# Partition sums of the modulation partials on TensorE, GpSimd's additions on VectorE, and a fourth raw weight buffer

## The chip, the core and the metric

The kernel runs on one core of a Trainium2 chip. The metric is the device time of one execution in microseconds (us). The engines are TensorE (PE, its weight loads PEld), VectorE (DVE), ScalarE (ACT), GpSimd (POOL) and SyncE (SP), which here only issues DMAs.

## The reference

One layer of a diffusion backbone in float32 over 128 context tokens and 256 latent tokens (384 columns together), width 2048:

```
mod = silu(c) @ w_ada + b_ada           # six parts of 2048: sh1, sc1, gt1, sh2, sc2, gt2; two vectors c (context, latent)
h   = RMSNorm(x) * (1 + sc1) + sh1
proj = h @ w_in                         # q, k, v, f, u, vg, three gates
merged = sum_i sigmoid(gate_i) * (branch_i @ w_br_i)     # attention, Fourier, spatial gating
x  += gt1 * RMSNorm(merged @ w_out)
h   = RMSNorm(x) * (1 + sc2) + sh2
x  += gt2 * RMSNorm(relu(h @ w1)^2 @ w2)
```

Weights lie in HBM in float32. `mod` is a product of two vectors with a matrix of 2048 x 12288.

## The kernel before

Weights come through one stream. `stream` is a list of entries of 512 KB: ("W", ...) entries are split into a high part (fp32r) and the low part that is left, ("D", ...) entries are handed to a function. `emit_dma` issues the entry's load on SP's queue into one of `R_BUFS` = 3 tiles `raw`; a tile comes free when the last instruction that reads it is done. `advance` takes the next entry. For a "W" entry it makes two half-tiles, each with a `whi` (ScalarE's cast, L71) and a `wlo` (VectorE's subtraction, L72, recorded under the helper's line L65); there are `H_BUFS` = 4 of each. `next_half` gives TensorE one half-tile, and looks ahead until two more are made. Each product is three matmuls (`mm3`, L575 to L577, or `mmB1`, L598 to L600), so a half-tile is 12 matmuls of 384 columns.

A "D" entry of `ada_dve` is worked on VectorE: for both vectors v it multiplies 128x512 weights by a column of `silT` (per-partition scalar) and adds to an accumulator (L271, L274), four instructions for an entry. After eight entries (2048 rows) the accumulator holds 128 partial sums of each column, one in each partition, which have still to be added over the partitions. These entries are mixed into the stream: sixteen of `CORR` ("v0" and "f": the shift's share of two projections) with the first main entries, twelve blocks `ADA(m, j)` of m = 2, 4, 3 with the gates and the output projection, four of m = 5 (gt2) with the first part of the MLP.

The sum over the partitions is GpSimd's `partition_all_reduce` (`all_sum`), which leaves it in all partitions. For m = 2, 3, 4 the result is wanted as a column (`modT`, features in partitions): a mask keeps the diagonal (`affine_select`) and `fin` reduces it on VectorE (L304). GpSimd also adds the gated branches (`br_evac`, L1059) and the squares of x before the MLP (`x2_d`, L1194).

The order on every engine is that of the program. After each half-tile `slot()` runs a task or two of the lists `late` (evacuations), `urgent` and `side`; `delayed` holds tasks that become urgent some slots later (`RED_AFTER`, `ADD_AFTER`).

Of the kernel before, what the change touches and what calls it, by code (L numbers as in the profile page):

```python
# [13 lines left out]
F32 = mybir.dt.float32  # L14
F32R = mybir.dt.float32r
# [20 lines left out]
def hybrid_layer_kernel(ctx: ExitStack, tc: tile.TileContext, I: dict, O: dict):  # L36
# [250 lines left out]
    def mod_done(m, j):  # L287
        s = slice(4 * j, 4 * j + 4)

        def one(v):  # L290
            def run():
                t = adr["t"][:, 1, j % 2, v, :]
                all_sum(t, accs[m, j][v])
                t3 = t.rearrange("p (n k) -> p n k", n=4)
                nc.gpsimd.affine_select(out=t3, in_=t3, pattern=[[0, 4], [1, P]], base=0, channel_multiplier=-1,
                                        compare_op=ALU.is_equal, fill=0.0)
                if v == 1:
                    accs.pop((m, j))
                    nc.gpsimd.load_library(library_config.standard)
            return run  # L300
# [11 lines left out]
        def tasks():  # L312
            delayed.append([RED_AFTER, [fin]])
            return [one(0), one(1)]
        return tasks
# [3 lines left out]
    def gt2_done(j):  # L319
        c = slice(512 * j, 512 * (j + 1))  # L320

        def one(v):
            def run():
                acc = accs[5, j][v]
                if "t" not in a2bc:
                    a2bc["t"] = area.tile([P, 2, D], F32, tag="a2", name="a2")
                a2 = a2bc["t"]
                if v == 0:
                    for q, src in enumerate((I["b_ada"][0:1, 5 * D + 512 * j:5 * D + 512 * (j + 1)],
                                             I["g_post_mlp"][0:1, c])):  # L330
                        a2bc[j, q] = tp.tile([P, 512], F32, tag="sq", name=f"bg{j}{q}")
                        nc.gpsimd.dma_start(out=a2bc[j, q], in_=src.to_broadcast([P, 512]))
                all_sum(a2[:, v, c], acc)
                if v == 1:
                    accs.pop((5, j))
                    if j == 3:
                        nc.gpsimd.load_library(library_config.standard)
# [12 lines left out]
    def corr_done(name):  # L350
        def one(v):
# [1010 lines left out]
```

## Time and profile before

| | us |
|---|---|
| median of 3 runs | 2242.39 (2242.16 to 2245.22) |
| profiled execution, first to last instruction | 2241.9 |
| TensorE busy | 2168.3 (97%) |
| VectorE busy | 1458.1 (65%) |
| ScalarE busy | 814.8 (36%) |
| GpSimd busy | 252.6 (11%) |

The profiled execution is 0.5 us shorter than the median, so its parts can be read as parts of the run's time. Its stretches are: to about 180 the first entries, to 420 the rest of q, k, v and the spatial gating, to about 1000 gates and branches (`g`, `b`), to 1148 the output projection (`y`), to 1211 the first blocks of the MLP while its input is made, then the MLP. Busy time of TensorE is modelled and matmuls overlap, so what its idle time and the granted clock tell is read by stretch. The clock column is the mean share of full speed that was granted: 1.00 is the 2.4 GHz level, 0.50 the 1.2 GHz one.

### The profile page before, as it was taken

To read this page: it belongs to the slowest core of one execution; us is meant where nothing else is said; L and a number is where in the kernel's file an instruction comes from. 1 tells how busy PE (TensorE), PEld (TensorE's weight loads), DVE (VectorE), ACT (ScalarE), POOL (GpSimd) and SP (SyncE) were. 2 spreads that over 40 slices of the span, in tenths; PEclk is the share of its full clock that TensorE was granted. 3 is DMA by queue.
4 is the path that set the end of the run, shared out by engine and by line. 5 is a ranking of instruction groups with operands and counts; after the bars stand their busy time and mean duration, and the time that the engine had idled before them with its cause. 6 is when DMAs were issued, how large, how long until landed. Compare 5 with 4: busy or idle time off the path is not lost.

```text
span 2241.9 us, 30677 instructions
## 1 busy us (share of the span) xinstructions
PE 2168.3 (97%) x11479; PEld 1988.6 (89%) x11479; DVE 1458.1 (65%) x2331; ACT 814.8 (36%) x1602; POOL 252.6 (11%) x167
## 2 busy tenths in 40 slices
PE   7999899999999998999999999999999999999998
PEld 3679888999899998998989988899889998899986
DVE  4445675558998898989977577787444444345454
ACT  3332334533223232323245443344333443334441
POOL 0000221011222122212212001111000000000000
PEclk9999999999999999999999999999999999999999
DMA  8897753336666765666634466665444444444452
GB/s 309 288 314 232 198 161 123 103 116 196 201 195 194 212 207 168 201 203 224 218 102 134 126 191 200 205 188 174 127 132 124 128 125 129 126 130 123 123 175 88
DMA packets 284405, 387.29 MB, mean 173 GB/s; under 512 B 16156, under 2 KB 184304, under 8 KB 283872
## 3 DMA queue, kind: packets, MB, share of 16 engines
q1 hardware_dynamic: 275952, 372.82, 53.6%
q10 hardware_dynamic: 6192, 6.77, 1.0%
q0 software_dynamic: 2112, 5.74, 0.9%
q8 instruction: 90, 1.47, 0.3%
q14 instruction: 59, 0.48, 0.1%
HBM read 377.94 MB, written 8.26 MB: 172 GB/s over the span
## 4 chain that ended last, share of the span: by engine, by line
PE 75%; DVE 9%; DMA 8%; issue 5%; ACT 1%; POOL 1%; DVEq 0%; ACTq 0%; POOLq 0%; SPq 0%
PE m L576 7%; PE m L577 7%; PE m L575 7%; PE z L599 7%; PE z L600 7%; PE z L598 7%; DMA raw<-in_w_in_dram 4%; DVE wlo L65 4%; PE g L577 3%; PE g L575 3%; PE g L576 3%; DVE adr L274 3%; DMA raw<-in_w_ada_dram 2%; PE sc L248 2%; PE ew L598 1%
## 5 line engine op out<-in xcount | busy, mean ns | idle before, releaser
L65 DVE TENSOR_TENSOR wlo<-raw,whi 128x512 fp32r<-128x512 f32 x908 | 649.7, 734 | 573.5 <-ACT whi L71 566.2
L71 ACT CAST whi<-raw 128x512 fp32r<-128x512 f32 x908 | 547.8, 620 | 1102.8 <-PE z L600 262.0
L598 PE MATMUL z<-whi,ff 128*128 128x512 f32 x720 | 280.1, 389 | 0.0
L599 PE MATMUL z<-wlo,ff 128*128 128x512 f32 x720 | 280.1, 389 | 0.0
L600 PE MATMUL z<-whi,ff 128*128 128x512 f32 x720 | 280.1, 389 | 0.0
L274 DVE SCALAR_TENSOR_TENSOR adr<-raw,silT,adr 128x512 f32<-128x512 f32 x360 | 266.8, 801 | 15.5 <-DMA raw<-in_w_ada_dram 15.4
L577 PE MATMUL g<-hA,wlo 128*128 128x384 f32 x768 | 261.5, 341 | 15.6 <-DVE wlo L65 15.3
L575 PE MATMUL g<-hA,whi 128*128 128x384 f32 x768 | 260.9, 340 | 10.5 <-ACT whi L71 10.5
L576 PE MATMUL g<-hA,whi 128*128 128x384 f32 x768 | 259.4, 338 | 0.0
L575 PE MATMUL m<-h2a,whi 128*128 128x386 f32 x512 | 175.1, 342 | 2.1 <-ACT h2a L1181 2.1
L576 PE MATMUL m<-h2a,whi 128*128 128x386 f32 x512 | 174.3, 340 | 1.1 <-DVE h2a L1185 1.0
L577 PE MATMUL m<-h2a,wlo 128*128 128x386 f32 x512 | 173.8, 339 | 0.0
L577 PEld LDWEIGHTS g<-hA,wlo 128*128 128x128 f32 x768 | 146.2, 190 | 22.1 <-DVE wlo L65 22.1
L600 PEld LDWEIGHTS z<-whi,ff 128*128 128x128 f32 x720 | 135.1, 188 | 28.0
L598 PEld LDWEIGHTS z<-whi,ff 128*128 128x128 f32 x720 | 135.1, 188 | 27.9
L599 PEld LDWEIGHTS z<-wlo,ff 128*128 128x128 f32 x720 | 135.1, 188 | 27.9
L575 PEld LDWEIGHTS g<-hA,whi 128*128 128x128 f32 x768 | 146.1, 190 | 11.5 <-ACT whi L71 11.4
L576 PEld LDWEIGHTS g<-hA,whi 128*128 128x128 f32 x768 | 146.2, 190 | 0.0
L281 POOL PARTITION_ALL_REDUCE adr<-adr x24 | 87.4, 3640 | 302.8 <-DVE adr L274 235.1
L576 PEld LDWEIGHTS m<-h2a,whi 128*128 128x128 f32 x512 | 97.3, 190 | 2.3 <-DVE h2a L1185 2.1
L575 PEld LDWEIGHTS m<-h2a,whi 128*128 128x128 f32 x512 | 97.1, 190 | 2.4 <-ACT h2a L1181 2.3
L577 PEld LDWEIGHTS m<-h2a,wlo 128*128 128x128 f32 x512 | 96.9, 189 | 0.0
(343 smaller groups left out, 3824.6 us busy)
## 6 DMA issues: line engine op xcount, KB each, us to landing
raw<-in_w_mlp_dram SPq DMA_DIRECT2D x244, 512.0 KB, 3.7
raw<-in_w_in_dram SPq DMA_DIRECT2D x156, 512.0 KB, 3.8
raw<-in_w_ada_dram SPq DMA_DIRECT2D x128, 512.0 KB, 4.5
erb<-in_w_ada_dram SPq DMA_DIRECT2D x37, 512.0 KB, 5.5
raw<-in_w_out_dram SPq DMA_DIRECT2D x32, 512.0 KB, 4.2
era<-in_w_ada_dram SPq DMA_DIRECT2D x27, 512.0 KB, 5.1
era<-in_w_in_dram SPq DMA_DIRECT2D x20, 512.0 KB, 5.4
raw<-in_w_br_a_dram SPq DMA_DIRECT2D x16, 512.0 KB, 3.6
```

The costliest lines, as they stand in the source:

```text
L65: eng.tensor_tensor(out=out, in0=a, in1=b, op=op)
L71: nc.scalar.copy(out=hi, in_=full)
L248: nc.tensor.matmul(ps[g:g + 2, :wd], silT[:, :, k], r, start=k < 4, stop=k >= KT - 4)
L274: nc.vector.scalar_tensor_tensor(out=acc[v], in0=r, scalar=vec[:, v, k:k + 1], in1=acc[v], op0=ALU.mult, op1=ALU.add)
L281: nc.gpsimd.partition_all_reduce(out, acc, P, bass_isa.ReduceOp.add)
L575: nc.tensor.matmul(out, wh, xh, start=start, stop=False)
L576: nc.tensor.matmul(out, wh, xl, start=False, stop=False)
L577: nc.tensor.matmul(out, wl, xh, start=False, stop=stop)
L598: nc.tensor.matmul(ps[t], xh, hi, start=first, stop=False)
L599: nc.tensor.matmul(ps[t], xh, lo, start=False, stop=False)
L600: nc.tensor.matmul(ps[t], xl, hi, start=False, stop=last_)
```

## The change

The sums over the partitions become matmuls with ones. For m = 2, 3, 4, `red` multiplies each 128x128 piece of an accumulator (as weights) by one column of ones: eight matmuls of one column leave the sums in a PSUM tile in the layout of `modT`, and `fin` adds the bias from there. For m = 5 and `CORR`, `sum_bc` multiplies a 128x128 of ones by the accumulator, 512 columns, and leaves the sum in all partitions; the following addition on VectorE reads it from PSUM. `red` becomes urgent four slots after the last accumulation. The additions of `br_evac` and `x2_d` go to VectorE. `R_BUFS` is 4. The accumulators of `CORR` and of m = 5 lie in other tiles, and no GpSimd library is loaded.

```
-    R_BUFS = 3
+    R_BUFS = 4
     H_BUFS = 4
-    RED_AFTER = 14
-    ADD_AFTER = 7
+    RED_AFTER = 4
...
-                delayed.append([1, on_done()])
+                delayed.append([RED_AFTER, on_done()])
...
-    def all_sum(out, acc):
-        nc.gpsimd.partition_all_reduce(out, acc, P, bass_isa.ReduceOp.add)
+    def sum_bc(acc):
+        pb = mis_tile("sum")
+        nc.tensor.matmul(pb, ones, acc, start=True, stop=True)
+        return pb
...
-        def one(v):
-            def run():
-                t = adr["t"][:, 1, j % 2, v, :]
-                all_sum(t, accs[m, j][v])
-                t3 = t.rearrange("p (n k) -> p n k", n=4)
-                nc.gpsimd.affine_select(out=t3, in_=t3, pattern=[[0, 4], [1, P]], base=0, channel_multiplier=-1,
-                                        compare_op=ALU.is_equal, fill=0.0)
...
+        def red():
+            pr = mis_tile(f"red{m}{j}")
+            for v, acc in enumerate(accs.pop((m, j))):
+                for n in range(4):
+                    nc.tensor.matmul(pr[:, 4 * v + n:4 * v + n + 1], acc[:, n * P:(n + 1) * P], ones[:, 0:1],
+                                     start=True, stop=True)
+            last["red"] = pr
 
         def fin():
             dst = modT[:, m, :, s]
-            nc.vector.tensor_reduce(out=dst, in_=adr["t"][:, 1, j % 2].rearrange("p v (n k) -> p v n k", n=4),
-                                    axis=AX.X, op=ALU.add)
-            tt(nc.vector, dst, dst, bc2(bT[:, m, s]), ALU.add)
+            tt(nc.vector, dst, last.pop("red")[:, 0:8].rearrange("p (v n) -> p v n", v=2), bc2(bT[:, m, s]), ALU.add)
...
-        return lambda: [one(0), one(1), nop, nop, nop, fin]
+        return lambda: [load, nop, nop, red(0), add(0), red(1), add(1), fin]
...
+        def red():
+            pc.extend(sum_bc(acc) for acc in accs.pop((name, 0)))
 
         def add():
             dst, after = evacuated[name]
             for t in range(NT):
-                tt(nc.vector, dst[:, t, :], dst[:, t, :], evacuated["t"][min(t, 1)], ALU.add)
+                tt(nc.vector, dst[:, t, :], pc[min(t, 1)], dst[:, t, :], ALU.add)
...
                 if gi:
-                    tt(nc.gpsimd, sigs[0, n], sigs[0, n], s, ALU.add)
+                    tt(nc.vector, sigs[0, n], sigs[0, n], s, ALU.add)
...
-            tt(nc.gpsimd, sq2, sq2, sq, ALU.add)
+            tt(nc.vector, sq2, sq2, sq, ALU.add)
```

GpSimd before, at the second pair of column blocks: the four additions of gated branches of this pair (`sig`; numbers are buffers), then the library's load and the first partition sum of the next block.

```order
L65 TENSOR_TENSOR sig_4382<-sig_4382,sig_4542 128x384
L65 TENSOR_TENSOR sig_4396<-sig_4396,sig_4556 128x384
L65 TENSOR_TENSOR sig_4382<-sig_4382,sig_4696 128x384
L65 TENSOR_TENSOR sig_4396<-sig_4396,sig_4710 128x384
L281 ISA
L281 ISA adr<-adr 128x512
```

None of these rows is left on GpSimd: the additions stand on VectorE, the sums on TensorE, and the mask and the library loads (the bare `ISA` rows) are gone.

VectorE before, at the same pair, from the half-tile behind the Fourier branch (`b_..4757` and `4758` are its two products):

```order
L65 TENSOR_TENSOR sig_4542<-b_1_0_4757,sig_4542 128x384
L65 TENSOR_TENSOR sig_4556<-b_1_1_4758,sig_4556 128x384
L65 TENSOR_TENSOR wlo_0_4852<-raw_4803,whi_0_4851 128x512
L65 TENSOR_TENSOR wlo_1_4856<-raw_4803,whi_1_4855 128x512
L65 TENSOR_TENSOR sig_4696<-b_1_0_4801,sig_4696 128x384
L65 TENSOR_TENSOR sig_4710<-b_1_1_4802,sig_4710 128x384
```

VectorE now, at the same place (`4755` and `4756` are those products):

```order
L64 TENSOR_TENSOR sig_4545<-b_1_0_4755,sig_4545 128x384
L64 TENSOR_TENSOR sig_4385<-sig_4385,sig_4545 128x384
L64 TENSOR_TENSOR modT<-red_4799,bT 128x2x4
L64 TENSOR_TENSOR a_93<-modT,vT 128x2x4
L64 TENSOR_TENSOR sig_4559<-b_1_1_4756,sig_4559 128x384
L64 TENSOR_TENSOR sig_4399<-sig_4399,sig_4559 128x384
L64 TENSOR_TENSOR wlo_0_4861<-raw_4763,whi_0_4860 128x512
L64 TENSOR_TENSOR wlo_1_4865<-raw_4763,whi_1_4864 128x512
L64 TENSOR_TENSOR sig_4699<-b_1_0_4808,sig_4699 128x384
L64 TENSOR_TENSOR sig_4385<-sig_4385,sig_4699 128x384
L64 TENSOR_TENSOR sig_4713<-b_1_1_4809,sig_4713 128x384
L64 TENSOR_TENSOR sig_4399<-sig_4399,sig_4713 128x384
```

Each product is now followed by an addition, and `fin` of the block m = 2, j = 0 (the rows that write `modT` and `a_93`) stands between them, where a reduce of 128x1024 stood some rows later.

TensorE at the same place, before: the last matmuls of the Fourier branch and the first of the next.

```order
L576 MATMUL b_1_1_4758<-oF,whi_1_4724 128x384
L577 MATMUL b_1_1_4758<-oF,wlo_1_4725 128x384
L575 MATMUL b_1_0_4801<-oC,whi_0_4767 128x384
L576 MATMUL b_1_0_4801<-oC,whi_0_4767 128x384
```

TensorE now:

```order
L568 MATMUL b_1_1_4756<-oF,whi_1_4727 128x384
L569 MATMUL b_1_1_4756<-oF,wlo_1_4728 128x384
L300 MATMUL red_4799<-ones,adr 128x1 x8
L567 MATMUL b_1_0_4808<-oC,whi_0_4765 128x384
L568 MATMUL b_1_0_4808<-oC,whi_0_4765 128x384
```

Eight one-column matmuls stand between two half-tiles, behind the half `wlo_1_4728`. VectorE makes that half behind the last accumulation of the block, as its rows now show:

```order
L278 SCALAR_TENSOR_TENSOR adr<-raw_4635,silT,adr 128x512 x4
L64 TENSOR_TENSOR wlo_0_4724<-raw_4641,whi_0_4723 128x512
L64 TENSOR_TENSOR wlo_1_4728<-raw_4641,whi_1_4727 128x512
L275 TENSOR_SCALAR adr<-raw_4677,silT 128x512 x2
```

The last row begins the next block, in the other pair of accumulators.

SP's queue before, at the first loads of the main stream (each row with the semaphores that it waits for: a DMA's, or VectorE's when a buffer has to come free):

```order
L97 DMA raw_1315<-in_w_in_dram 128x4x256
L97 DMA raw_1321<-in_w_in_dram 128x2x512
L97 DMA raw_1363<-in_w_in_dram 128x4x256 [waits DMAHW0_49]
L97 DMA raw_1522<-in_w_in_dram 128x4x256 [waits DMAHW6_49,DMAHW3_49,DVE_49]
L97 DMA raw_1530<-in_w_in_dram 128x2x512 [waits DMAHW7_49,DMAHW4_49,DVE_49]
L97 DMA raw_1566<-in_w_in_dram 128x4x256 [waits DMAHW5_49,DMAHW0_49,DVE_49]
```

SP's queue now:

```order
L95 DMA raw_1315<-in_w_in_dram 128x4x256
L95 DMA raw_1321<-in_w_in_dram 128x2x512
L95 DMA raw_1363<-in_w_in_dram 128x4x256 [waits DMAHW0_49]
L95 DMA raw_1417<-in_w_in_dram 128x4x256 [waits DMAHW1_49]
L95 DMA raw_1524<-in_w_in_dram 128x2x512 [waits DMAHW6_49,DMAHW4_49,DVE_49]
L95 DMA raw_1531<-in_w_in_dram 128x4x256 [waits DMAHW7_49,DMAHW5_49,DVE_49]
```

The fourth load no longer waits for VectorE, and each later one waits for the buffer that is released one load earlier than before.

## Rows read from the trace of the kernel before

**Rows 1.** Stretches (us): busy time and (count) of each engine, granted clock, DMA share, GB/s.
```profile
0.00:180.00 180.00, 165.13 (x878) 111.12 (x879) 83.56 (x204) 67.42 (x120) 3.99 (x13) 1.00 0.87 296
180.00:300.00 120.00, 109.94 (x600) 104.20 (x599) 80.69 (x133) 34.71 (x70) 20.41 (x19) 0.97 0.71 210
300.00:540.00 240.00, 239.57 (x1345) 226.59 (x1344) 143.51 (x258) 100.93 (x211) 27.95 (x23) 1.00 0.44 134
540.00:1150.00 610.00, 576.66 (x3221) 563.45 (x3219) 531.73 (x757) 181.31 (x337) 141.50 (x76) 0.98 0.65 198
1150.00:1215.00 65.00, 58.56 (x316) 55.91 (x316) 53.91 (x102) 34.06 (x78) 20.50 (x19) 0.95 0.39 116
1215.00:2241.90 1026.90, 1018.40 (x5130) 927.29 (x5128) 564.67 (x880) 396.35 (x790) 38.24 (x17) 1.00 0.47 144
```

**Rows 2.** What TensorE waited for: total us, times, longest; 540 to 1150, then 180 to 300.
```profile
PE g L577 <- DVE wlo L65: 15.3, 15, 3.7
PE g L575 <- ACT whi L71: 10.5, 2, 8.6
...
PE q L575 <- ACT whi L71: 5.9, 3, 3.7
```

**Rows 3.** ScalarE's waits in 540 to 1150, the one on GpSimd.
```profile
ACT mH L1063 <- POOL sig L65: 25.4, 6, 12.5
```

**Rows 4.** GpSimd's groups in 540 to 1150: busy us, mean ns | idle before.
```profile
L281 POOL PARTITION_ALL_REDUCE adr<-adr x24 | 87.4, 3640 | 302.8 <-DVE adr L274 235.1 <-ACT whi L71 49.2 <-issue 12.6
L65 POOL TENSOR_TENSOR sig<-sig,sig 128x384 f32<-128x384 f32 x28 | 34.5, 1254 | 173.3 <-DVE sig L65 158.7 <-issue 7.5 <-DVE wlo L65 7.1
```

**Rows 5.** VectorE's groups in 540 to 1150, same columns.
```profile
L274 DVE SCALAR_TENSOR_TENSOR adr<-raw,silT,adr 128x512 f32<-128x512 f32 x338 | 251.7, 804 | 15.0 <-DMA raw<-in_w_ada_dram 14.8
L65 DVE TENSOR_TENSOR wlo<-raw,whi 128x512 fp32r<-128x512 f32 x266 | 200.4, 791 | 48.2 <-ACT whi L71 46.0 <-PE g L577 1.3
L271 DVE TENSOR_SCALAR adr<-raw,silT 128x512 f32<-128x512 f32 x22 | 30.3, 1419 | 0.4 <-DMA raw<-in_w_ada_dram 0.4
L65 DVE TENSOR_TENSOR sig<-b,sig 128x384 f32<-128x384 f32 x42 | 21.3, 547 | 0.0
L304 DVE TENSOR_REDUCE modT<-adr 128x8 f32<-128x1024 f32 x12 | 14.5, 1210 | 0.0
```

**Rows 6.** Same tiles, whole span: duration ns min/median/max, first and last start us.
```profile
L274 DVE SCALAR_TENSOR_TENSOR adr<-raw,silT,adr x360: 733/744/2728, 508.3 to 1111.8; 128x512 f32<-128x512 f32 x180
L271 DVE TENSOR_SCALAR adr<-raw,silT x24: 473/1062/2468, 507.5 to 1071.7; 128x512 f32<-128x512 f32 x24
...
L65 DVE TENSOR_TENSOR wlo<-raw,whi x908: 674/691/2733, 187.5 to 2201.1; 128x512 fp32r<-128x512 f32 x182
```

**Rows 7.** Seven stretches without GpSimd work: the last one, and their sum.
```profile
1080.00:1110.00 30.00, 29.29 (x166) 28.26 (x166) 28.08 (x49) 9.46 (x18) 0.00 (x0) 1.00 0.74 230
...
sum 180.00, PE 178.91 PEld 176.96 DVE 157.45 ACT 57.10 POOL 0.24; mean PE 25.56 PEld 25.28 DVE 22.49 ACT 8.16 POOL 0.03
```

**Rows 8.** Three pieces at the lower clock: the first and the last.
```profile
659.00:668.00 9.00, 5.27 (x17) 5.28 (x18) 7.95 (x10) 1.46 (x3) 4.69 (x2) 0.62 0.51 164
...
968.00:975.00 7.00, 5.23 (x21) 4.91 (x20) 6.13 (x10) 1.91 (x4) 1.54 (x2) 0.76 0.59 179
```

**Rows 9.** TensorE in time around `colsum`: start us, us, what.
```profile
1207.89 0.34 PE L577 MATMUL m<-h2c,wlo 128*128 128x386 f32 x1
1208.07 0.72 PE L1126 MATMUL r<-ones,sq 128*128 128x1 f32 x6
...
1208.92 0.33 PE L576 MATMUL m<-h2c,whi 128*128 128x386 f32 x1
```

**Rows 10.** TensorE in time around L491, same columns.
```profile
24.57 0.81 PE L491 MATMUL pr<-dg,ones 128*128 128x384 f32 x2
25.31 0.60 PE L248 MATMUL sc<-erb,silT 128*2 128x512 f32 x2
```

**Rows 11.** DMA before the main stream, columns as in group 1.
```profile
173.00:186.00 13.00, 13.00 (x76) 13.00 (x76) 5.76 (x13) 7.32 (x15) 1.54 (x3) 1.00 0.11 34
```

More of the change, by code (lines that the diff above doesn't have):

```diff
@@ L8 @@
 import concourse.tile as tile
-from concourse import bass_isa, library_config
 from concourse import mybir
@@ L260, in run @@
                     if "t" not in adr:
-                        adr["t"] = area.tile([P, 2, 2, 2, 512], F32, tag="a2", name="adr")
-                    accs[m, j] = [adr["t"][:, 0, j % 2, v, :] for v in range(2)]
-                else:
-                    accs[m, j] = [tp.tile([P, 512], F32, tag="ada", name=f"ada{m}_{j}_{v}", bufs=3) for v in range(2)]
+                        adr["t"] = area.tile([P, 2, 2, 512], F32, tag="a2", name="adr")
+                    accs[m, j] = [adr["t"][:, j % 2, v, :] for v in range(2)]
+                elif m == 5:
+                    if "t" not in a2bc:
+                        a2bc["t"] = area.tile([P, 2, D], F32, tag="a2", name="a2")
+                    accs[m, j] = [a2bc["t"][:, v, 512 * j:512 * (j + 1)] for v in range(2)]
+                else:
+                    if "t" not in evacuated:
+                        evacuated["t"] = area.tile([P, 2, 2, 512], F32, tag="B2a", name="corr")
+                    accs[m, j] = [evacuated["t"][:, int(m == "f"), v, :] for v in range(2)]
             acc = accs[m, j]
@@ L310, in fin @@
                 plus1_times(A2, 4, g_pre_mlp, s)
[L312 to L315, printed above, removed]
+        return lambda: [red, fin]
     a2bc = {}
@@ L320, in gt2_done, with load, red, add @@
         c = slice(512 * j, 512 * (j + 1))
-        def one(v):
-            def run():
[L324 to L337, printed above, removed]
+        def load():
+            for q, src in enumerate((I["b_ada"][0:1, 5 * D + 512 * j:5 * D + 512 * (j + 1)],
+                                     I["g_post_mlp"][0:1, c])):
+                a2bc[j, q] = tp.tile([P, 512], F32, tag="sq", name=f"bg{j}{q}")
+                nc.gpsimd.dma_start(out=a2bc[j, q], in_=src.to_broadcast([P, 512]))
+        def red(v):
+            def run():
+                a2bc["ps"] = sum_bc(accs[5, j][v])
+            return run
+        def add(v):
+            def run():
+                tt(nc.vector, a2bc["t"][:, v, c], a2bc.pop("ps"), a2bc[j, 0], ALU.add)
             return run
         def fin():
-            for q, op in enumerate((ALU.add, ALU.mult)):
-                tt(nc.vector, a2bc["t"][:, :, c], a2bc["t"][:, :, c],
-                   a2bc[j, q].unsqueeze(1).to_broadcast([P, 2, 512]), op)
-        return lambda: [one(0), one(1), nop, nop, nop, fin]
+            accs.pop((5, j))
+            tt(nc.vector, a2bc["t"][:, :, c], a2bc["t"][:, :, c],
+               a2bc[j, 1].unsqueeze(1).to_broadcast([P, 2, 512]), ALU.mult)
+        return lambda: [load, nop, nop, red(0), add(0), red(1), add(1), fin]
     def ADA(m, j):
@@ L350, in corr_done @@
     def corr_done(name):
-        def one(v):
-            return lambda: all_sum(evacuated["t"][v], accs[name, 0][v])
+        pc = []
+        def red():
+            pc.extend(sum_bc(acc) for acc in accs.pop((name, 0)))
         def add():
@@ L356, in add @@
             for t in range(NT):
-                tt(nc.vector, dst[:, t, :], dst[:, t, :], evacuated["t"][min(t, 1)], ALU.add)
-            accs.pop((name, 0))
+                tt(nc.vector, dst[:, t, :], pc[min(t, 1)], dst[:, t, :], ALU.add)
             after()
-        def tasks():
-            delayed.append([ADD_AFTER, [add]])
-            return [one(0), one(1)]
-        return tasks
+        return lambda: [red, nop, add]
     evacuated = {}
@@ L704, in hybrid_layer_kernel @@
     oA = area.tile([P, 2, 8, 386], F32R, tag="B1", name="oA")
-    oF = area.tile([P, 2, 4, 386], F32R, tag="B2a", name="oF")
+    oF = {}
     at2 = area.tile([P, 8 * 386], F32, tag="B2b", name="att2")
@@ L793, in run @@
             assert f_ready
+            if not oF:
+                oF["t"] = area.tile([P, 2, 4, 386], F32R, tag="B2a", name="oF")
             c = slice(g * P, (g + 1) * P)
@@ L826, in run @@
                 tt(nc.vector, fo[:, t0 + n - 1:t0 + h:-1], cc, ss, ALU.subtract)
-            put_o(fo, oF, g)
+            put_o(fo, oF["t"], g)
         return run
@@ L1038, in hybrid_layer_kernel @@
     src_m = lambda p, k: mt[p][:, k, :]
[L1039 removed]
+    src_o = lambda p, k: oA[:, p, k, :] if k < 8 else oF["t"][:, p, k - 8, :] if k < 12 else gt["o"][:, p, k - 12, :]
     sigs = {}
```

6 lines of the change are left out of this document (removed).

## The prediction

> **What bounds the kernel now.** I read the stretches first, to see who is full where [rows 1]. TensorE (PE) is full in two of them: 239.6 of 240 us busy from 300 to 540, and all but 8.5 of 1026.9 us from 1215 on. It waits in three: the start (14.9 us, which no edit touches), 180 to 300 (10.1 us), and 540 to 1150, the gates, branches and output projection (33.3 us idle). Only that third stretch also has VectorE (DVE) nearly full, 531.7 of 610 us, beside 141.5 us of GpSimd (POOL). So the next view is what ended TensorE's waits [rows 2]: in 540 to 1150 it is the low weight halves that VectorE makes (`wlo`, L65, 15 waits of gate matmuls, 15.3 us) and the high halves of ScalarE (`whi`, L71, 10.5 us in two waits, one of 8.6). The 8.6 has GpSimd behind it: ScalarE itself waited 25.4 us in this stretch for sums of gated branches from GpSimd, 12.5 us once [rows 3], and every later `whi` stands behind that instruction.
>
> Then GpSimd's and VectorE's groups in the same stretch [rows 4, 5]. The three costliest VectorE groups are slower here than the same forms elsewhere [rows 6]: 338 accumulations at a mean of 804 ns against a median of 744, 266 `wlo` at 791 against 691, 22 first products at 1419 against a minimum of 473. That is 338 x 0.060 + 266 x 0.100 + 22 x 0.946 = 20.3 + 26.6 + 20.8 = 67.7 us of VectorE time, lost beside 141.5 us of GpSimd, 0.48 us for each us. Where GpSimd is quiet, TensorE hardly waits: in seven stretches of 180 us with 0.24 us of GpSimd it is idle 1.1 us [rows 7].
>
> One more loss: after a wait the granted clock falls to the lower level, and TensorE is busy but at half pace. At full pace a matmul of this stage takes 29.29 / 166 = 0.176 us [rows 7]. Three pieces of the stretch have a mean granted clock of 0.62 to 0.76; in the first, 17 matmuls took 5.27 us, 2.3 us too long, in the last, 21 took 5.23, 1.5 too long [rows 8]. About 6 us in the three. So 33.3 + 6 = 39 us is all that 540 to 1150 can give.
>
> **The change, part by part.**
> *What leaves GpSimd in 540 to 1150.* All 24 all-reduces, their masks and 28 of the 32 branch sums [rows 4]. VectorE loses 67.7 us of slowdown and twelve reduces (14.5 us [rows 5]), and gains 28 adds of 128x384. The same form costs it 547 ns [rows 5], so 15.3 us. It comes to 531.7 - 67.7 - 14.5 + 15.3 = 465 us of some 600: no longer late on the mean. ScalarE's wait for GpSimd goes too, since the add now stands ahead of `hi` on VectorE, one 0.55 us instruction. I expect TensorE to wait as it does beside a quiet GpSimd: 1.1 / 180 of some 570 us, 3.5 us. The worst of those stretches has 0.71 us in 30 [rows 7], which would be 13.5. So 39.2 - 3.5 = 35.7 us come back; the bounds are 25.7 and 39.2.
>
> *What is added on TensorE.* Twelve `red` of eight one-column f32 matmuls each. The nearest rows are the three of `colsum` [rows 9], same shape and type: from the ordinary matmul before them (1207.89) to the second one after them (1208.92) is 1.03 us, two ordinary steps of which are 0.35, so 0.68 us for three, 0.226 each, and 96 cost 21.7 us. They lie wholly in 540 to 1150. Twelve `sum` matmuls of 128x512 f32 with ones: the nearest is the 128x384 one of L491, which runs as two records and holds TensorE from 24.57 to 25.31, 0.74 us [rows 10]; by columns 0.99 for 512, so 11.8 us. Unscaled it would be 8.9; at two whole records of 0.60, as the next row's 512-column ones have, 14.4. I take 11.8, the same kind of operand. Four lie before 540 and eight behind 1215, where TensorE has no idle time to hide them. Together 33.5 us.
>
> *The waits that these make.* `red` waits for VectorE's last accumulation, and all of TensorE is behind it. It is issued four half-tiles after that accumulation, and the low halves that TensorE used in between stand behind the accumulation in VectorE's order, so it is done: 0. `fin` on VectorE waits for `red`, with the next `wlo` behind it; TensorE then has two half-tiles in stock, 24 matmuls or 4.2 us, against `fin` and two `wlo` of 0.69: 0 as well, while VectorE has spare time. If that cover is gone, each `red` shows as a wait of TensorE for `wlo`.
>
> *The fourth raw buffer.* Around 180 the DMA engines are idle: 0.11 busy from 173 to 186 [rows 11], since the three raws allowed behind the early entries have been asked for. A fourth now lands there. Sixteen `CORR` entries stand among the first 26 main ones, so 1.6 raws go with the 24 matmuls (4.2 us) of one, and one raw more is a lead of 2.6 us, against three waits of 5.9 us in `q`, the longest 3.7 [rows 2]. The stretch has 10.1 us idle and a granted clock of 0.97 [rows 1], two half-pace pieces that I put at 3 us. At most 13 us, at least nothing, since the DMA engines are 0.71 busy there and some transfers would only queue. I take 6. In 540 to 1150 its help is in the 35.7.
>
> *The additions behind 1150.* Fifteen adds of 128x384 move to VectorE, 15 x 0.547 = 8.2 us, into 65 us of which it works 53.9 [rows 1]. On GpSimd they were 15 x 1.25 us [rows 4], 19 of its 20.5 us there, and by the rate above these cost VectorE 0.48 x 19 = 9. Zero, within 3 either way. (The `bg` rows of m = 5 stay on GpSimd's queue, issued four slots ahead of the addition that reads them, in a stage where VectorE works 564.7 of 1026.9 us: 0.)
>
> *Sum.* 2241.9 - 35.7 - 6 + 33.5 + 0 = 2233.7 us of the profiled execution; the runs' median lies 0.5 above its span, so **2234 us**. With every bound at its good end 2241.9 - 39.2 - 13 + 30.6 - 3 = 2217, at its bad end 2241.9 - 25.7 + 36.1 + 3 = 2255. The change swaps some 42 us of waiting for some 33 us of matmuls.
>
> **The rivals.**
> *TensorE pays and is not paid back: slower.* The 33.5 us are certain; the return is not. If VectorE stays late, because the adds fall on the very slots at the branch blocks' ends where it has most to do (two products, two adds and two low halves in three half-tiles), half of the 39.2 us comes back: 2241.9 - 19.6 - 0 + 33.5 = 2256, or 2250 with the buffer's 6. It decides at a return of 33.5 us over both stretches. For it: VectorE is the last releaser in most waits [rows 2]. Against: 465 of 600 us, and the quiet stretches, where VectorE is as busy. The Trainium skill has a rule on this side (GPSIMD Engine Reference, Engine selection): a reduction along the partitions is given to GpSimd. By it the sums stay where TensorE pays nothing; this case's row has 3.64 us for one 128x512 all-reduce against 1.8 us for two accumulators' `red`, so the trace has the cheaper sum on TensorE, though on the engine that is full.
> *The buffer gives nothing: no change.* The DMA engines are the limit from 188 to 270, and the rest goes as forecast: 2241.9 - 35.7 + 33.5 = 2239.7, 2240 in the runs.
> *Everything comes back.* 39 and 13 us, 2241.9 - 52.2 + 33.5 = 2223.
> *`red` waits for VectorE.* If the four half-tiles are too few, twelve waits as long as the longest for `wlo` now, 3.7 us [rows 2], 44 us: over 2270. The order of the instructions speaks against it.
>
> **How the numbers follow.** The forecast has 0.50, everything back 0.10, the buffer without effect 0.23, slower 0.17 (0.03 of it the wait of `red`). Differences under 0.2% (4.5 us) can hardly be told from none here. Faster (under 2238) is the forecast and the good case, 0.60; the same is the third, 0.23; slower 0.17. The likeliest case's own range is 2226 to 2238. A range from 2222 to 2250 leaves out the far end of the slower case and a little below.
>
> **What would show it.** In the profile after: VectorE's `wlo` and `adr` groups at 0.69 and 0.75 us in all stages; no ScalarE wait for a branch sum; TensorE idle under 14 us in 540 to 1150 and no piece at the lower clock there; `red` records near 0.11 us apart and `sum` near 1 us; TensorE's waits between 200 and 270 shorter by half. The prediction is wrong if `wlo` still ends waits of TensorE by more than 15 us in that stretch, if a `red` or `sum` costs twice its row, or if `raw` lands no earlier around 225.

## The result and the profile after

The changed kernel takes **2206.32 us** (median of 4 runs, 2205.68 to 2206.93) against 2242.27 of the kernel before beside it: a ratio of 0.9842, 95% interval 0.9828 to 0.9856, 36 us. The forecast was 2234 in a range of 2222 to 2250: the direction was right, the size was not. The profiled execution spans 2203.9 us.

The page after: TensorE's busy time, and the chain that ended last by engine (before: 75% PE, 9% DVE, 8% DMA).

```profile
PE 2175.5 (99%) x11695; PEld 2007.6 (91%) x11695; DVE 1376.3 (62%) x2370; ACT 826.2 (37%) x1602; POOL 41.6 (2%) x60
...
PE 97%; DMA 1%; DVE 1%; issue 1%; ACT 0%; POOL 0%; DVEq 0%; POOLq 0%; ACTq 0%
```

Stretches after, columns as in [rows 1]. Since all comes earlier, the second row, 528.50 to 1109.50, holds about the work that stood in 540 to 1150.

```profile
180.00:300.00 120.00, 118.81 (x662) 112.66 (x662) 88.41 (x150) 39.86 (x78) 14.92 (x18) 1.00 0.73 230
528.50:1109.50 581.00, 580.78 (x3413) 580.49 (x3411) 464.92 (x773) 192.45 (x337) 0.00 (x0) 1.00 0.67 207
...
1150.00:1215.00 65.00, 65.00 (x393) 64.42 (x392) 39.20 (x76) 37.02 (x92) 2.37 (x3) 1.00 0.46 138
```

TensorE is idle 0.2 of 581 us, at full clock, and VectorE works 464.9 where the forecast had 465. The longest of what TensorE waited for from 180 to 1150 (total us, times, longest), against the groups of [rows 2]:

```profile
PE m L567 <- ACT h2a L1174: 2.1, 1, 2.1
PE r L1123 <- POOL st L186: 1.2, 1, 1.2
PE k L569 <- DVE wlo L64: 0.9, 1, 0.9
PE pa L882 <- DVE s L873: 0.4, 1, 0.4
```

VectorE's groups from 540 to 1150 after, the same as in [rows 5]: 745, 687 and 479 ns where they had 804, 791 and 1419; the 28 branch additions (`sig<-sig,sig`) cost 558 ns each.

```profile
L278 DVE SCALAR_TENSOR_TENSOR adr<-raw,silT,adr 128x512 f32<-128x512 f32 x330 | 225.9, 745 | 0.0
L64 DVE TENSOR_TENSOR wlo<-raw,whi 128x512 fp32r<-128x512 f32 x276 | 186.1, 687 | 104.7 <-ACT whi L70 104.6
...
L64 DVE TENSOR_TENSOR sig<-sig,sig 128x384 f32<-128x384 f32 x28 | 15.6, 558 | 1.0
L275 DVE TENSOR_SCALAR adr<-raw,silT 128x512 f32<-128x512 f32 x22 | 9.6, 479 | 0.0
```

The new matmuls on TensorE in time (start us, us): a `red` among branch matmuls, then a `sum` in the MLP.

```profile
547.64 0.34 PE L568 MATMUL b<-oF,whi 128*128 128x384 f32 x1
547.82 0.34 PE L569 MATMUL b<-oF,wlo 128*128 128x384 f32 x1
547.99 1.84 PE L300 MATMUL red<-ones,adr 128*128 128x1 f32 x16
549.69 0.42 PE L567 MATMUL b<-oC,whi 128*128 128x384 f32 x1
549.95 0.34 PE L568 MATMUL b<-oC,whi 128*128 128x384 f32 x1
...
1313.66 0.40 PE L592 MATMUL z<-whi,ff 128*128 128x512 f32 x1
1313.90 1.02 PE L286 MATMUL sum<-a,ones 128*128 128x512 f32 x2
1314.36 0.80 PE L590 MATMUL z<-whi,ff 128*128 128x512 f32 x1
1314.99 0.40 PE L591 MATMUL z<-wlo,ff 128*128 128x512 f32 x1
```

Ordinary starts are 0.175 us apart here and 0.227 in the MLP. From 547.82 to 549.95 are 2.13 us with two ordinary steps in them, so a `red` costs 1.78, twelve 21.4. From 1313.66 to 1314.99 are 1.33, less two steps 0.88 for a `sum`: eight cost 7.0. The four of `CORR`, in two pairs at 243 and 317 us, cost 1.7 a pair.

**Where the 38 us between the two profiled executions lie.** I follow the first matmul of each group: `k`, `v`, `b` (first branch), `r1c` (first one behind the output projection), `z`.

| stretch | before | after | gain | of it paid to the new matmuls |
|---|---|---|---|---|
| start to k | 186.9 | 185.9 | 1.0 | |
| k to v | 106.5 | 94.1 | 12.4 | 1.7 |
| v to b | 186.6 | 188.5 | -1.9 | 1.7 |
| b to r1c | 668.7 | 639.8 | 29.0 | 21.4 |
| r1c to z | 155.0 | 150.6 | 4.4 | |
| z to the end | 938.2 | 945.1 | -6.9 | 7.0 |

So b to r1c returned 29.0 + 21.4 = 50.4 us, where the forecast had 35.7 and called 39 all that there was.

### The profile page after: what moved, and what is told of

Its sections match the earlier page's. It is cut to its first block, busy times and chain, and to the rows that moved or that the text cites. A ratio compares the mean times of both kernels' runs of the same rounds, so it can differ in the third digit from the quotient of the medians.

```text
span 2203.9 us, 30938 instructions
## 1 busy us (share of the span) xinstructions
PE 2175.5 (99%) x11695; PEld 2007.6 (91%) x11695; DVE 1376.3 (62%) x2370; ACT 826.2 (37%) x1602; POOL 41.6 (2%) x60
## 4 chain that ended last, share of the span: by engine, by line
PE 97%; DMA 1%; DVE 1%; issue 1%; ACT 0%; POOL 0%; DVEq 0%; POOLq 0%; ACTq 0%
PE m L568 8%; PE m L567 8%; PE m L569 8%; PE z L592 7%; PE z L591 7%; PE z L590 7%; PE g L567 6%; PE g L568 6%; PE g L569 6%; PE b L567 2%; PE b L568 2%; PE b L569 2%; PE y L567 2%; PE y L569 2%; PE y L568 2%; PE sc L246 2%
## 5 line engine op out<-in xcount | busy, mean ns | idle before, releaser
L64 DVE TENSOR_TENSOR wlo<-raw,whi 128x512 fp32r<-128x512 f32 x908 | 617.6, 690 | 628.1 <-ACT whi L70 624.9
L70 ACT CAST whi<-raw 128x512 fp32r<-128x512 f32 x908 | 560.2, 621 | 1072.3 <-PE z L592 294.4
L569 PE MATMUL g<-hA,wlo 128*128 128x384 f32 x768 | 256.9, 335 | 0.0
L278 DVE SCALAR_TENSOR_TENSOR adr<-raw,silT,adr 128x512 f32<-128x512 f32 x360 | 246.4, 745 | 0.0
L567 PE MATMUL m<-h2b,whi 128*128 128x386 f32 x256 | 87.8, 343 | 0.0
```

The source lines that it names most:

```text
L64: eng.tensor_tensor(out=out, in0=a, in1=b, op=op)
L70: nc.scalar.copy(out=hi, in_=full)
L278: nc.vector.scalar_tensor_tensor(out=acc[v], in0=r, scalar=vec[:, v, k:k + 1], in1=acc[v], op0=ALU.mult, op1=ALU.add)
L567: nc.tensor.matmul(out, wh, xh, start=start, stop=False)
L569: nc.tensor.matmul(out, wl, xh, start=False, stop=stop)
```

## The experiments

Three theories. **Contention**: GpSimd's work slows VectorE's instructions, and TensorE waits for its low halves. **Buffer** (later: stock): three raws are too few, and the fourth takes the waits away whoever is late. **Chain** (later: order): ScalarE stood behind GpSimd's additions, these behind all-reduces, and every high half behind ScalarE.

The table has every kernel's median and, from its trace, the two stretches in which they differ. "Lost" is b to r1c less its `red` less 618.4 us, which is what the changed kernel takes there without its `red` (639.8 - 21.4). Measured again beside these kernels, the kernel before had medians of 2240.48, 2239.28, 2238.44 and 2239.63, so medians taken beside different ones compare to within some 4 us. "Lost" comes from one execution each; a_modpool and a_modpool4, and a_dummy and a_dummy1, turn out to have the same order of events nearly throughout (below), and differ in it by 2.2 and 2.8 us.

| kernel | raws | on GpSimd | median us | k to v | b to r1c | red | lost |
|---|---|---|---|---|---|---|---|
| before | 3 | sums, branch additions | 2242.27 | 106.5 | 668.7 | 0 | 50.4 |
| b_sigdve | 3 | sums | 2233.07 | 102.1 | 660.7 | 0 | 42.3 |
| b_nomod | 3 | additions; sums of 2 to 4 left out | 2191.99 | 102.1 | 621.3 | 0 | 3.0 |
| a_r3 | 3 | none | 2218.39 | 104.4 | 639.8 | 21.4 | 0.0 |
| a_sigmod | 4 | sums of 2 to 4, additions | 2211.42 | 92.8 | 644.1 | 0 | 25.8 |
| a_modpool | 4 | sums of 2 to 4 | 2206.22 | 93.7 | 639.4 | 0 | 21.1 |
| a_modpool4 | 4 | the same, issued later | 2205.80 | 93.9 | 637.3 | 0 | 18.9 |
| a_noreduce | 4 | the same, no reduce | 2202.17 | 94.8 | 634.3 | 0 | 16.0 |
| a_dummy | 4 | unused sums | 2211.87 | 94.5 | 644.6 | 21.4 | 4.8 |
| a_dummy1 | 4 | unused sums, issued earlier | 2211.32 | 93.9 | 647.4 | 21.4 | 7.6 |
| a_sigpool | 4 | additions | 2206.69 | 92.9 | 640.0 | 21.4 | 0.3 |
| a_x2pool | 4 | squares of x | 2210.33 | 92.8 | 639.8 | 21.4 | 0.0 |
| a_double | 4 | none; new matmuls twice | 2257.69 | 94.6 | 681.7 | 42.8 | 20.5 |
| after | 4 | none | 2206.32 | 94.1 | 639.8 | 21.4 | 0.0 |
| a_modgt2 | 4 | sums of 2 to 5 | 2198.41 | 93.6 | 637.2 | 0 | 18.8 |
| a_mix | 4 | sums of 5, nine blocks of 2 to 4 | 2189.98 | 93.6 | 629.5 | 5.3 | 5.8 |
| a_mixc | 4 | the same and CORR | 2186.26 | 91.2 | 629.9 | 5.3 | 6.2 |

**Three raws** (on the changed kernel)

```
-    R_BUFS = 4
+    R_BUFS = 3
```

> The changed kernel with three raw weight buffers, as before; sums and additions stay where the change put them. Contention theory (GpSimd's all-reduces and sums slowed VectorE, which makes the low halves that TensorE waits for in 540 to 1150): only the 12 to 14 us that came back before 293 us are lost, so 2218 to 2221 us, and the gates, branches and output projection stay as full as with four, TensorE idle there within 2 us of what it is after the change. Buffer theory (three raws were too few in 540 to 1150 too, and the fourth is what filled that stretch): the waits for low halves come back there, and the time is above 2245. If the early stretch was freed by the other edits and not by the buffer: within 4 us of 2206.

2218.39 us, 12 lost, as contention had it. Its stretches:

```profile
180.00:300.00 120.00, 112.82 (x614) 105.77 (x613) 81.35 (x136) 36.33 (x73) 13.82 (x17) 0.97 0.70 211
540.00:1090.00 550.00, 550.00 (x3232) 550.00 (x3231) 454.77 (x748) 176.26 (x318) 0.00 (x0) 1.00 0.69 213
```

With GpSimd silent, three raws are enough from 540 on: TensorE has no idle time in 550 us. The fourth is worth 104.4 - 94.1 = 10.3 us from k to v.

**Unused sums on GpSimd** (on the changed kernel, in `red`, into a spare part of `adr`)

```
+            for v, acc in enumerate(parts):
+                t = adr["t"][:, 1, j % 2, v, :]
+                all_sum(t, acc)
+                t3 = t.rearrange("p (n k) -> p n k", n=4)
+                nc.gpsimd.affine_select(out=t3, in_=t3, pattern=[[0, 4], [1, P]], base=0, channel_multiplier=-1,
+                                        compare_op=ALU.is_equal, fill=0.0)
+            nc.gpsimd.load_library(library_config.standard)
```

> The changed kernel with GpSimd's old work of the twelve modulation blocks put back as work that nobody uses: 24 all-reduces, their masks and the library loads run into tiles that nothing reads, while the ones matmuls still make the results. Contention theory: VectorE loses about 0.48 us for each of some 110 us of GpSimd, 50 us, in a stretch where it had 130 us to spare, so low halves are late in places: 15 to 35 us are lost, 2221 to 2241, with the median accumulation beside GpSimd near 0.80 us and not 0.745. Theory of the waits (before, engines stood behind results that GpSimd made late, and its use of the memory cost little): nobody waits, so within 4 us of 2206.

2211.87: 5.5 lost, under what contention had and over what the other theory had. **The sums of 2, 3 and 4 back on GpSimd**, with mask and reduce as before:

```
-        return lambda: [red, fin]
+        def tasks():
+            delayed.append([14, [fin]])
+            return [one(0), one(1)]
+        return tasks
```

> The changed kernel with the sums of modulation blocks 2, 3 and 4 back on GpSimd (all-reduce, mask, VectorE's reduce, its last step 14 half-tiles later); four raws, branch sums on VectorE. TensorE saves twelve red, 21.4 us. Contention theory: 15 to 35 us are lost as in the run with unused all-reduces, so between 2200 and 2220, no clear gain over 2206. Theory of the buffer (with a fourth raw the stretch no longer feels GpSimd): the 21.4 us are all saved, 2185.

2206.22, the time of the changed kernel. Two groups of VectorE from 540 to 1110, first with unused sums, then with the real ones:

```profile
L65 DVE TENSOR_TENSOR wlo<-raw,whi 128x512 fp32r<-128x512 f32 x261 | 194.2, 769 | 60.7 <-ACT whi L71 60.5
L276 DVE TENSOR_SCALAR adr<-raw,silT 128x512 f32<-128x512 f32 x22 | 25.1, 1182 | 0.0
```

```profile
L65 DVE TENSOR_TENSOR wlo<-raw,whi 128x512 fp32r<-128x512 f32 x261 | 197.6, 789 | 42.1 <-ACT whi L71 41.7
...
L276 DVE TENSOR_SCALAR adr<-raw,silT 128x512 f32<-128x512 f32 x22 | 21.5, 1015 | 0.0
```

The contention is there in both and about as large, but one loses 4.8 us and the other 21.1. I look at the same place in both traces. VectorE's rows there are alike: the all-reduce begins at 636.53 with the real sums and at 638.20 with the unused ones, and in both the next block's first products start 1.65 us later and the low halves behind them 8.73 us later. TensorE's rows are not alike, first with the real sums on GpSimd:

```profile
642.14 0.33 PE L580 MATMUL g<-hA,whi 128*128 128x384 f32 x1
642.32 0.34 PE L581 MATMUL g<-hA,whi 128*128 128x384 f32 x1
646.00 0.69 PE L582 MATMUL g<-hA,wlo 128*128 128x384 f32 x1 [3.34 <-DVE wlo L65]
646.48 0.52 PE L580 MATMUL g<-hA,whi 128*128 128x384 f32 x1
646.80 0.52 PE L581 MATMUL g<-hA,whi 128*128 128x384 f32 x1
```

then with `red` on TensorE and the unused sums beside it:

```profile
644.94 0.33 PE L581 MATMUL g<-hA,wlo 128*128 128x384 f32 x1
645.11 1.84 PE L305 MATMUL red<-ones,adr 128*128 128x1 f32 x16
...
647.67 0.44 PE L581 MATMUL g<-hA,wlo 128*128 128x384 f32 x1 [0.26 <-DVE wlo L65]
```

In the first, TensorE waits 3.34 us and goes on at 0.32 us a step, the lower clock; in the second it has `red` to do while the low half is late. At this place the wait is a moment of some 3 us behind a block's end, not a mean.

**Only the branch additions back**

```
-                    tt(nc.vector, sigs[0, n], sigs[0, n], s, ALU.add)
+                    tt(nc.gpsimd, sigs[0, n], sigs[0, n], s, ALU.add)
```

> The changed kernel with only the 32 additions of the gated branches back on GpSimd, which has nothing else to do there. Chain theory (ScalarE stood behind GpSimd's additions in its order, and all its high halves with it): ScalarE's wait for GpSimd's sum comes back at the branch blocks, 4 to 12 us are lost, 2210 to 2218. Contention theory: 32 additions of 1.25 us slow VectorE by 0.48 x 40 = 19 us and spare it 32 x 0.55 = 18 us: within 3 us of 2206; the 8.6 us wait of before came from additions queued behind all-reduces, and these are gone.

2206.69, no change: the chain costs nothing by itself where no all-reduce stands in it. **The reverse on the kernel before**:

```
-                    tt(nc.gpsimd, sigs[0, n], sigs[0, n], s, ALU.add)
+                    tt(nc.vector, sigs[0, n], sigs[0, n], s, ALU.add)
```

> The kernel before with one edit: the 32 branch additions on VectorE; all sums stay on GpSimd, three raws. After the first four runs the contention theory stands as a cause of some 5 us beside four raws and the fourth raw as worth 12 us in the early stretch, which leaves most of the 50 us of 540 to 1150 to explain. Order theory: before, these additions stood behind 3.6 us all-reduces in GpSimd's order, ScalarE behind them, and every high half behind ScalarE, so that this one edit gives back 15 to 30 us, 2210 to 2226. Stock theory: with three raws any slow VectorE instruction empties TensorE's stock, whoever is late first, so this edit gives 8 us or less, 2232 to 2241.

2233.07 against 2239.28, 6 us: what the stock theory had, not order. In this trace no engine waits for a result of GpSimd from 540 to 1110, and yet 42.3 us are lost. What TensorE waits for are low halves, and what is slow is VectorE, whose first products here took 1524 ns where the changed kernel has 479:

```profile
PE g L577 <- DVE wlo L65: 17.9, 14, 3.7
L271 DVE TENSOR_SCALAR adr<-raw,silT 128x512 f32<-128x512 f32 x22 | 32.7, 1524 | 0.5 <-DMA raw<-in_w_ada_dram 0.5
```

**The sums of 2 to 4 left out** of the kernel before:

```
-                all_sum(t, accs[m, j][v])
-                t3 = t.rearrange("p (n k) -> p n k", n=4)
-                nc.gpsimd.affine_select(out=t3, in_=t3, pattern=[[0, 4], [1, P]], base=0, channel_multiplier=-1,
-                                        compare_op=ALU.is_equal, fill=0.0)
...
-            nc.vector.tensor_reduce(out=dst, in_=adr["t"][:, 1, j % 2].rearrange("p v (n k) -> p v n k", n=4),
+            nc.vector.tensor_reduce(out=dst, in_=adr["t"][:, 0, j % 2].rearrange("p v (n k) -> p v n k", n=4),
```

> The kernel before with the 24 all-reduces, masks and library loads of modulation blocks 2, 3 and 4 left out (VectorE's reduce reads the unsummed partials, so these results lack the sum over partitions); branch additions stay on GpSimd, three raws. TensorE gets no red. All of the 540 to 1150 loss hangs on the all-reduces (by contention, or by what queues behind them): the 50 us come back, 2187 to 2195. Order theory with the additions late by themselves: 15 us or more of it stay, above 2205.

2191.99: 47 us. The loss hangs on the all-reduces (with their masks and library loads); additions and three raws stayed, and 3.0 us are lost:

```profile
540.00:1090.00 550.00, 549.37 (x3147) 546.78 (x3146) 475.28 (x748) 177.54 (x328) 33.12 (x28) 1.00 0.70 216
```

**Additions and sums both on GpSimd, four raws** (on a_modpool, the edit of a_sigpool)

> The changed kernel with both the branch additions and the sums of blocks 2, 3 and 4 back on GpSimd; four raws. Beside the run with these sums alone back (2206.2) the additions stand behind all-reduces again. Order theory: ScalarE's wait for GpSimd's additions returns, 15 to 30 us more, 2221 to 2236. Stock theory: with four raws the wait is covered, 2206 to 2212.

2211.42, with the long wait of ScalarE of [rows 3] back, and longer:

```profile
ACT mH L1069 <- POOL sig L65: 29.0, 6, 15.5
```

So the order costs 4.7 us of lost time (25.8 against 21.1) with four raws and 8.1 (50.4 against 42.3) with three. Kernels with three and with four raws and the same work on GpSimd in this stretch differ by 21 to 25 us (42.3 and 21.1, 50.4 and 25.8), and without all-reduces there (a_r3 and the changed kernel) by none. The first two pairs differ also in `CORR`, m = 5 and the squares, whose work lies outside the stretch; no run changed the buffer alone beside the all-reduces.

**All-reduces issued later** (four half-tiles after the last accumulation, not one)

```
-                delayed.append([1 if m in (2, 3, 4) else RED_AFTER, on_done()])
+                delayed.append([RED_AFTER, on_done()])
```

> The changed kernel with the sums of blocks 2, 3 and 4 back on GpSimd as in the run before, but started four half-tiles after the last accumulation and not one. In that run the long TensorE waits (646, 841, 989 us) stand beside all-reduces that ran together with the next block's first products, two of them of 2.5 us. If it is this overlap of a burst of VectorE work with an all-reduce that costs the 21 us, a later start spares part of it: 2190 to 2200, faster than the changed kernel. If it is the mean load of VectorE, the time stays within 4 us of 2206.

2205.80, the number of the mean load. But the edit did not do what it was meant to. GpSimd has nothing else to do here and begins as soon as the accumulation is done, wherever the all-reduce is issued. At the place shown above, first in a_modpool, then here:

```profile
636.53 4.84 POOL L286 PARTITION_ALL_REDUCE adr<-adr  x1 [41.03 <-DVE adr L279]
638.18 3.47 DVE L276 TENSOR_SCALAR adr<-raw,silT 128x512 f32<-128x512 f32 x2
```

```profile
637.97 4.84 POOL L286 PARTITION_ALL_REDUCE adr<-adr  x1 [41.03 <-DVE adr L279]
639.62 3.48 DVE L276 TENSOR_SCALAR adr<-raw,silT 128x512 f32<-128x512 f32 x2
```

The first products follow 1.65 us behind the all-reduce's start in both, so the run decides nothing between the burst and the mean load. **The unused sums issued earlier**:

```
+                if m in (2, 3, 4):
+                    delayed.append([1, [unused(m, j, 0), unused(m, j, 1)]])
                 delayed.append([RED_AFTER, on_done()])
```

> The changed kernel with the 24 unused all-reduces, masks and library loads put one half-tile after a block's last accumulation, where the kernel before has them, instead of beside red. The run with them beside red lost 5.5 us, the run with the real sums on GpSimd lost 21 us of waits at the same 54 us of slower VectorE. Theory of the covered stall: beside red TensorE has 1.8 us of other work while VectorE is slow, so the stall was hidden; three half-tiles earlier it is not, and 10 to 18 us are lost, 2216 to 2224. Theory of the load: what cost the 21 us are the twelve reduces of 1.2 us and TensorE's faster pace, not the place: 2210 to 2214 again.

2211.32, lost 7.6: the number of the load, not of the covered stall. But this edit moved nothing either: the all-reduce begins 1.65 us ahead of the first products in a_dummy (638.20 and 639.85) and 1.66 ahead here (637.91 and 639.57), and `red` still stands four half-tiles behind the block's end, where the late low half comes. **VectorE's reduces left out** is the better one:

```
-            nc.vector.tensor_reduce(out=dst, in_=adr["t"][:, 1, j % 2].rearrange("p v (n k) -> p v n k", n=4),
-                                    axis=AX.X, op=ALU.add)
-            tt(nc.vector, dst, dst, bc2(bT[:, m, s]), ALU.add)
+            tt(nc.vector, dst, adr["t"][:, 1, j % 2, :, 0:4], bc2(bT[:, m, s]), ALU.add)
```

> The run with the sums of blocks 2, 3 and 4 back on GpSimd, but VectorE's twelve reduces of 128x1024 are left out: one column of each masked sum is taken in their place, so these modulations are incomplete. If the reduces' 14.5 us of VectorE work were part of what cost the 21 us of waits, 6 us or more come back: 2200 or less. If the waits are those of low halves beside the all-reduces, which TensorE's 1.8 us of red covered where both ran: 2203 to 2207, with the waits near 646, 841 and 989 us as before.

2202.17, between the two: the reduces account for some 3 to 5 of the 21 us, and 16 stay, with waits of 2.32, 3.40 and 1.74 us at 646, 839 and 985.

**Each new matmul twice**

```
-                for n in range(4):
+                for n in (0, 1, 2, 3, 0, 1, 2, 3):
```

> The changed kernel with each red and each sum matmul issued twice (the second overwrites the first with the same values). Price theory: the sums cost what stands in the rows, 12 x 1.78 + 2 x 1.71 + 8 x 0.88 = 31.8 us, all on the path: 2238. If part of it lies in time that TensorE would wait anyway: below 2230. With the forecast's 33.5 us: 2240.

2257.69, 51 more and not 32. The doubled `red` takes 3.57 us, as it should (1068.00 to 1071.92 less two steps), but then:

```profile
1068.00 0.33 PE L570 MATMUL y<-mH,wlo 128*128 128x384 f32 x1
1068.17 3.63 PE L301 MATMUL red<-ones,adr 128*128 128x1 f32 x32
1071.66 0.42 PE L568 MATMUL y<-mH,whi 128*128 128x384 f32 x1
1071.92 0.33 PE L569 MATMUL y<-mL,whi 128*128 128x384 f32 x1
...
1072.79 0.53 PE L568 MATMUL y<-mH,whi 128*128 128x384 f32 x1
1073.11 0.53 PE L569 MATMUL y<-mL,whi 128*128 128x384 f32 x1
...
1075.99 0.43 PE L569 MATMUL y<-mL,whi 128*128 128x384 f32 x1
```

About ten steps of 0.32 instead of 0.175 us follow, at the 1.2 GHz level, some 1.7 us behind each `red` (20.5 over the stretch) without any idle time. The price of the sums stands as 31.8; this extra is the doubling's own, since behind the single `red` of the changed kernel no piece at the lower clock stands.

**The squares of x back on GpSimd**

```
-            tt(nc.vector, sq2, sq2, sq, ALU.add)
+            tt(nc.gpsimd, sq2, sq2, sq, ALU.add)
```

> The changed kernel with only the 15 additions of squares behind 1150 us back on GpSimd. The forecast had this edit at nothing, the two traces at 4.4 us between the first r1c and the first z. If the 4.4 come from these additions: 2209 to 2212. If from how long the clock stayed low after the wait at 1113 us, or from the freed GpSimd elsewhere: 2204 to 2208.

2210.33, 4.0 us more, and r1c to z takes 154.4 us instead of 150.6: the MLP's input (`h2a`, `h2b`, `h2c`), made by VectorE, is late again, 2.5 us in seven waits (0.2 in one in the changed kernel):

```profile
PE m L568 <- DVE h2a L1178: 1.9, 4, 0.8
...
PE m L568 <- DVE h2b L1178: 0.4, 2, 0.2
...
PE m L568 <- DVE h2c L1178: 0.2, 1, 0.2
```

**Better versions.** All block sums on GpSimd (on a_modpool; m = 5 as in the kernel before):

```
-        return lambda: [load, nop, nop, red(0), add(0), red(1), add(1), fin]
+        return lambda: [one(0), one(1), nop, nop, nop, fin]
```

> The changed kernel with the sums of modulation blocks 2, 3, 4 and 5 back on GpSimd as the kernel before has them; only the two correction sums stay on TensorE; four raws, additions on VectorE. If the sums of block 5 lie under a stage where VectorE has time to spare, the 7.0 us of their eight matmuls are saved beside the 2206.2 of the run with blocks 2, 3 and 4 back: 2198 to 2200. If GpSimd's slowing of VectorE reaches TensorE in the feed-forward stage too: 2203 to 2207.

2198.41. Then three of the twelve blocks on TensorE, where the waits were:

```
+    BY_PE = ((2, 2), (4, 2), (3, 1))
...
+        return (lambda: [red, fin]) if (m, j) in BY_PE else tasks
```

> As the run with blocks 2, 3, 4 and 5 on GpSimd, but three of the twelve blocks of 2, 3 and 4 have their sums on TensorE: the third, seventh and tenth, those beside whose all-reduces TensorE had its longest waits (646, 841, 989 us; 8.5 us idle and some 7 at the lower clock). Stall-by-place theory: nine blocks save 9 x 1.78 = 16 us on TensorE and some 5 us of waits stay, 7 us from block 5: 2185 to 2191, the best so far. If the waits move to other blocks when these are taken out: 2194 to 2200.

2189.98; of the waits for low halves in 540 to 1110, 11.4 us in a_modgt2, 2.9 stay:

```profile
PE g L593 <- DVE wlo L65: 2.9, 6, 1.0
```

With `CORR` on GpSimd too:

```
-        return lambda: [red, nop, add]
+        def tasks():
+            delayed.append([7, [add]])
+            return [one(0), one(1)]
+        return tasks
```

> The best run so far (2190.0, all but three blocks' sums on GpSimd) with the two correction sums back on GpSimd too, added seven half-tiles later as in the kernel before. They cost 1.7 us each on a TensorE that is full there: 2186 to 2188 if GpSimd's all-reduces reach no wait between 230 and 320 us, where VectorE works 88 of 120 us; 2190 or more if they do.

**2186.26 us**, a ratio of 0.9762 (0.9747 to 0.9777) to the kernel before, and 18 to 20 us faster than the changed kernel (18 by the two ratios, 20 by the medians).

## Why the prediction was off

*What bounds it, right.* VectorE made late by GpSimd's all-reduces was the cause: take them away and the loss goes, with three raws and GpSimd's additions still there (b_nomod); leave them, and most of it stays though nobody waits for GpSimd (b_sigdve). The additions queued behind the all-reduces were the smaller part, 8 us.

*The price on TensorE, right.* 31.8 us for 33.5: `red` 21.4 for 21.7, the twelve `sum` 10.4 for 11.8. *VectorE's load, right*: 464.9 for 465. *The new waits, right*: none for `red`; VectorE's for it (3.1 us in six) are not seen by TensorE.

*The step that failed:* "33.3 + 6 = 39 us is all that 540 to 1150 can give." 50.4 came back, and the term that was too small is the 33.3: I took TensorE's modelled idle time for all that its waits cost. The starts of its matmuls show more. From the first `b` to the first `r1c` of the kernel before I count what each start lost against a step of 0.174 us.

The 27 waits that the profile shows cost 37.2 us where it shows 32.7. A matmul is shown 0.34 us long while starts are 0.174 apart, so the last one before a wait covers 0.16 us of it (642.32 to 646.00 in a_modpool above is 3.68 us, one step 0.17, so 3.5 lost, where 3.34 is shown). Another 52 starts come 0.05 to 0.30 us late with no wait shown, 6.6 us in all. One of them is the low half at 579.68, which starts 0.44 us behind the matmul before it, and the next one follows after 0.28:

```profile
579.24 0.34 PE L576 MATMUL g<-hA,whi 128*128 128x384 f32 x1
579.68 0.45 PE L577 MATMUL g<-hA,wlo 128*128 128x384 f32 x1
579.96 0.34 PE L575 MATMUL g<-hA,whi 128*128 128x384 f32 x1
```

So the waits cost 43.8 us. The lower clock was sized right: 42 starts in the three pieces lost 6.4 us, where I had put 6. (The stretch's granted clock of 0.98 times its 610 us would be 9 to 15 us, but that share counts time in which TensorE did nothing, as in this row, where it is busy 0.20 of 8.78 us at a clock of 0.68.)

```profile
869.40:878.18 8.78, 0.20 (x2) 0.00 (x0) 0.54 (x2) 1.08 (x3) 0.98 (x1) 0.68 0.12 40
```

Together 50.2. The forecast also left 3.5 us of waits standing, of which 0.2 were left. That makes the 14.7 us between 35.7 and 50.4, half of the forecast's error of 28 (29.8 in spans: the forecast put the median 0.5 us above the span, and it lies 2.4 above); most of the rest is the buffer's 8 and the last additions' 4, below. The Trainium skill (Perfetto Trace Analysis, Identifying the Most-Contended Engine) warns of matmul busy time and has the weight loads' busy share in its place. The row agrees: PEld was busy 563.45 of 610 us before [rows 1], 46.6 short, which is nearer to 50.4 than the 33.3 that I took.

*The fourth buffer, mis-sized:* 6 us; the stretch returned 12.4 + 1.7 = 14.1, of which the run with three raws gives the buffer 10.3, within its bound of 13. Two other kernels with three raws and `CORR`'s sums on GpSimd took 102.1 there, so some 4 of before's 106.5 may belong to that one execution.

*The additions behind 1150, mis-sized:* 0 with 3 either way, measured 4.0. I weighed VectorE's time in the sum; what counted was that single pieces of the MLP's input were late.

*The rivals.* "Everything comes back" came nearest, but its 52 us was set too low by the same step: 14.1 + 50.4 + 4.0 came back. "The buffer gives nothing" and "`red` waits" fell. The slower rival fell by its number, yet it was right that sums on TensorE are dear: beside four raws, twelve `red` pay 21.4 us for 21.1 us of waits. The rule of the Trainium skill that I weighed against this (GPSIMD Engine Reference, Engine selection) is borne out for nine of twelve blocks, m = 5 and `CORR`, and not for the three beside whose all-reduces TensorE waited longest: a_mixc, which follows it but for these three, is the fastest kernel here.

*What stays open.* The two gains are not separate: removing the all-reduces returns 47 us at three raws and 21 to 26 at four, so a share for each edit depends on the order in which they are made. That `red` covers late low halves is seen at one place and agrees with a_noreduce, but no run put `red` elsewhere, and no run moved three other blocks to TensorE. When the all-reduces start was never varied, since two edits meant to do it did not. The fourth raw alone in the kernel before was not run.

## What to carry to other kernels

Before a sum is moved to the engine that is full, try what makes its waits harmless (one more buffer): here kernels with the fourth buffer and the sums still on GpSimd lost 21 to 26 us where those with three lost 42 to 50, and moving the twelve block sums then broke even. Take the loss of a stretch from the starts of its matmuls or from the weight loads' busy time, not from modelled idle time, and do not multiply a stretch's granted clock by its length where it holds idle time. Look at where the waits stand: moving the sums at the three longest ones gained 8 us, and the matmuls that filled those moments were paid for by the waits. And read from the trace whether an edit moved what it was meant to move.

## What the runs showed of the hardware

- Behind each `red` of the changed kernel, sixteen one-column f32 records (1.78 us), TensorE went on at 0.174 us a step, the 2.4 GHz level. Behind the doubled ones of a_double, 32 records (3.57 us) with TensorE never idle, ten or eleven steps of 0.32 us followed, the 1.2 GHz level (granted clock 0.86 from 1065 to 1077).
- A small f32 matmul goes by records: two of 0.112 us for one column; a 128x512 one with ones costs 0.86 to 0.88 us in all.
- VectorE's first products, 479 ns alone, took up to 2.46 us beside an all-reduce (a_modpool, at 638.18). The Trainium skill (SBUF — State Buffer, SBUF: two separate sides) has GpSimd and those VectorE instructions that run in a two-port mode, or that read two operands from SBUF while GpSimd reads SBUF too, take a shared port pair by turns, the loser blocked for the whole instruction. The trace agrees that single instructions are held up for about 2 us, but not that one all-reduce is one turn: beside the all-reduce of 4.84 us from 636.53 in a_modpool, VectorE finished three instructions that had begun after it, two low halves that took 1.28 us together and a product of 2.46. The profile's spans on GpSimd are rough, so how the turns fall within the 4.84 us stays open.
